# Three attention steps between the projection tiles of layer 0, and sums of squares that stay on TensorE

## The chip, the cores and the metric

One core of one Trainium2 chip runs the program. Its engines work from queues of their own: TensorE (PE, with its weight loads shown as PEld), VectorE (DVE), ScalarE (ACT), GpSimd (POOL) and the queue that issues transfers (SP). The metric is device microseconds of one execution, the median of three runs: 2119.75 (2119.36 to 2120.94).

## The reference, cut to what matters

Two layers (DEPTH 2) over 512 latent tokens with 256 context tokens ahead of them, 1024 wide. Each layer: adaLN modulation, RMSNorm, one input projection for three head groups, an output projection, then SwiGLU. The three groups are latent attention (mla, 4 heads), neighbourhood attention (na, 4 heads of 64) and a bidirectional gated DeltaNet (4 heads of 128). The parts that the change touches:

```
def l2_norm(x):
    return xf * lax.rsqrt(jnp.sum(xf * xf, axis=-1, keepdims=True) + EPS)

# gated_deltanet_mixer, for latents and for context:
qkv = silu(centred_depthwise_conv(t[..., :3 * DN_W], conv_w))
g = -exp(a_log) * softplus(a + dt_bias)
return l2_norm(q), l2_norm(k), v, g, sigmoid(b)

# chunk_gated_delta_rule, chunks of 64 tokens:
gc = cumsum(g)
decay = exp(gc_i - gc_j)                  # lower triangle
L = strict_lower(kb @ k.T) * decay        # kb = k * beta
tinv = inverse(L + I)
... a scan over the chunks with tinv, k_tail, q_dec and a_intra

# the gate projection z enters at the very end:
out = rms_norm(o, g_out) * silu(z)
```

## The kernel before, in words

A tile framework orders the instructions of each engine by simulating a timeline, within the order of the program text, data, and the buffers of its pools. Every large product is fp32 split in two parts: a weight tile is loaded (raw tile wr, two buffers, line 215), ACT casts its high part wh (line 216), POOL subtracts for the low part wl (line 217), and PE makes three products (hh with wh, hl with wh, hh with wl). Projections land in PSUM tiles acc_in (512 latent and 256 context columns of a head at a time).

The modulation columns (ada_cols, lines 222 to 242) load a tile wada, which has the same tag and the same two buffers as wr, multiply it (acc_ada), copy the row adarow and turn it by two small products (tr_ada). In layer 0, 24 of them run beside attention: two for each of the 12 steps (ADA).

A layer goes: the decay and gate inputs; then projections and convolutions of the DeltaNet's keys (conv, whose silu products dn_k are lines 504 and 506); norms("k"); the gates of six token chunks (each has k_tp, gram, dp on PE; gul, Ec on POOL; E on ACT); values, q and norms("q"); na's keys, queries and values; and the tail.

The order around the change:

- g (scal) comes off a DVE chain of softplus steps (lines 539 to 547). Five matmuls turn it into cumulative decays (tile gc, line 104 by the profile, since every mm has that line), then exps on ACT.
- norms (lines 568 to 591): ACT squares a head (sqd). PE multiplies it with a 32-column selector as the stationary operand, so that each head's sums land as rows of a PSUM tile (ssq). DVE copies the rows (line 581), PE transposes them by blocks of 128 (ss_tp, line 585), DVE copies each result into the statistics (stq or st4, line 586).
- After the gates, strips of the triangular matrices go through DRAM (d_inv); inverse(x) builds the block inverses from them: mix (transposes on DVE), pp and yq (products on PE), p, X and Y (copies).
- The tail of projections follows the string TAIL: z a gate projection tile (do_z, head by head), k the latent attention's key and value tile, q its query tile with ms_q (mean squares of sqs), n one step of neighbourhood attention (s_na scores, softmax, tp_na transposes copied to pt, o_na). Layer 0 has "zzzzkq", layer 1 "kznqznznz".
- A loop then runs the remaining attention steps, each with DNS[l] steps of the DeltaNet scan (yp, sp, oa) and, in layer 0, two modulation columns.

Of the kernel before, what the change touches and what calls it, by code (L numbers as in the profile page):

```python
# [9 lines left out]
F32 = mybir.dt.float32  # L10
F32R = mybir.dt.float32r
AF = mybir.ActivationFunctionType
ALU = mybir.AluOpType
# [4 lines left out]
P = 128  # L18
# [16 lines left out]
BN = dict(S=2, T=3)  # L35
BM = dict(S=3, T=3)
ADA = ([2] * 12, [])
DNS = ([1, 0, 0] + [1] * 4 + [0] + [1] * 12, [2, 2, 2, 1, 1, 2, 3] + [2] * 11)
ADA_T = "T"
EB = dict(e=5)  # L40
BO = {512: 3, 256: 2}
EB_TAG = {}
PRE0, LATE = True, ()
ROW = lambda S, V: S.copy
HLP = ([(k, 1) for k in range(8)], [], [(k, 1) for k in (0, 2, 4, 6, 7)], [])
TAIL = ["zzzzkq", "kznqznznz"]
INV = ((4, 3), (4, 3))
WV = ((6,), (23,))
MR = 2
# [51 lines left out]


def mm(nc, out, lhsT, rhs, start=True, stop=True):
    nc.tensor.matmul(out, lhsT, rhs, start=start, stop=stop)  # L104


def mm3(nc, out, l, r, start=True, stop=True):
# [255 lines left out]
def layer(tc, nc, a, l, es_x, xT, env, nx):  # L363
# [185 lines left out]
    S.activation(out=beta, in_=ab[:, :, 8:16], func=AF.Exp, scale=-1.0)  # L549
    V.tensor_scalar(out=beta, in0=beta, scalar1=1.0, scalar2=None, op0=ALU.add)  # L550
    V.reciprocal(out=beta, in_=beta)

    egc, etail, egl = sc6(), sc6(), sc6()
    tp = eb("gc")
    gf = g.rearrange("p c x -> p (c x)")
    for i, nm in enumerate(("u_f", "u_b", "v_f", "v_b", "ones")):
        mm(nc, tp[:, 48 * i:48 * i + 48], C(nm), gf)
    tpv = lambda i: tp[:, 48 * i:48 * i + 48].rearrange("p (c x) -> p c x", x=8)
    for d in range(2):
        ds_ = slice(4 * d, 4 * d + 4)  # L560
        S.activation(out=egc[:, :, ds_], in_=tpv(d)[:, :, ds_], func=AF.Exp)
        S.activation(out=etail[:, :, ds_], in_=tpv(2 + d)[:, :, ds_], func=AF.Exp)
    S.activation(out=egl, in_=tpv(4), func=AF.Exp)
    V.tensor_scalar(out=sml[:, 12:13], in0=sml2[:, 19:20], scalar1=0.5, scalar2=None, op0=ALU.mult)

    t2 = lambda nm: sb.tile([P, 512], F32, tag="t2", name=nm, bufs=5)

    def norms(nm, t_, stat, rk, w_ctx):

        cs = both if w_ctx else (LAT,)  # L570
        ps_ = [eb(f"ssq{ci}") for ci in range(len(cs))]
        for h in range(4):
            for ci, cols in enumerate(cs):
                w = cols.stop - cols.start
                sq = t_("sqd")
                S.activation(out=sq[:, :w], in_=hv[nm](h)[:, cols], func=AF.Square)
                mm(nc, ps_[ci][32 * h:32 * h + 32, 0:w], C("sel0"), sq[:, :w])
        rows = [t_(f"ssq_{ci}") for ci in range(len(cs))]
        for ci, cols in enumerate(cs):
            w = cols.stop - cols.start  # L580
            V.tensor_copy(out=rows[ci][:, 0:w], in_=ps_[ci][:, 0:w])
        n = 6 if w_ctx else 4
        for c in range(n):
            tp = eb("ss_tp")
            PE.transpose(tp[:, 0:P], rows[c // 4][:, (c % 4) * P:(c % 4 + 1) * P], ident)
            V.tensor_copy(out=stat[:, c], in_=tp[:, 0:P].rearrange("p (h x) -> p h x", h=4)[:, :, 0])
        V.tensor_scalar(out=stat[:, 0:n], in0=stat[:, 0:n], scalar1=EPS, scalar2=None, op0=ALU.add)
        S.activation(out=rk[:, 0:n], in_=stat[:, 0:n], func=AF.Ln)
        S.activation(out=rk[:, 0:n], in_=rk[:, 0:n], func=AF.Exp, scale=-0.5)

# [1 line left out]
        conv("k", h, kT[:, h])  # L592
    st4, rk = [sb.tile([P, 6, 4], F32, name=nm) for nm in ("st4", "rk")]
    norms("k", t2, st4, rk, True)
    irk = sc3()
    tt(out=irk, in0=st4, in1=rk, op=ALU.mult)
    rk2 = sc3()
# [249 lines left out]
    def attention():  # L847
        for pair in range(2):
            gm = gms[pair]
            o_na = sn.tile([P, T], F32, tag="o_na", name="o_na", bufs=1)  # L850
            grid = lambda t: t[:, LAT].rearrange("p (r c) -> p r c", c=GW)
            qh, ql, kh, kl = nqh[:, pair], nql[:, pair], nkh[:, pair], nkl[:, pair]
            for qt in range(nT // P):
                is_ctx = qt >= 4
                tok = slice(qt * P, (qt + 1) * P)
                c0 = (0, 8, 24, 32, 0, 0)[qt]
                var = (0, 1, 1, 2, 0, 0)[qt]
                vb = ((0, 1), (6, 7), (7, 8), (2, 3), (), ())[qt] + (4, 5)
                lo_ = 256 if is_ctx else 0
                pts = []  # L860
                for j in range(2):
                    hs = slice(64 * j, 64 * j + 64)
                    cutk = lambda t: grid(t)[hs, :, c0:c0 + 32].rearrange("p r (b c) -> p b r c", b=2)
                    s_ = att_bank("s_na")
                    if not is_ctx:
                        mm3(nc, s_[:, 0:256], (qh[hs, tok], ql[hs, tok]), (cutk(kh), cutk(kl)))
                    mm3(nc, s_[:, 256:512], (qh[hs, tok], ql[hs, tok]), (kh[hs, CTX], kl[hs, CTX]))
                    st_ = sn.tile([P, 8], F32, tag="st", name="st", bufs=4)
                    pr = sn.tile([P, 512], F32, tag="pr", name="pr", bufs=2)
                    V.reduce_max(out=st_[:, 0:1], in_=s_[:, 256:512], axis=AX.X)  # L870
                    if is_ctx:
                        V.tensor_scalar(out=st_[:, 2:3], in0=st_[:, 0:1], scalar1=-1.0, scalar2=None, op0=ALU.mult)
                    else:
                        V.tensor_tensor_reduce(out=pr[:, 0:256], in0=s_[:, 0:256], in1=gm[:, j, var].rearrange("p b r c -> p (b r c)"),
                                               scale=1.0, scalar=NEG, op0=ALU.add, op1=ALU.max, accum_out=st_[:, 1:2])
                        V.tensor_scalar(out=st_[:, 2:3], in0=st_[:, 0:1], scalar1=st_[:, 1:2], scalar2=-1.0, op0=ALU.max, op1=ALU.mult)
                        S.activation(out=pr[:, 0:256], in_=pr[:, 0:256], func=AF.Exp, bias=st_[:, 2:3], accum_out=st_[:, 3:4])
                    S.activation(out=pr[:, 256:512], in_=s_[:, 256:512], func=AF.Exp, bias=st_[:, 2:3], accum_out=st_[:, 4:5])
                    if is_ctx:
                        V.reciprocal(out=st_[:, 5:6], in_=st_[:, 4:5])  # L880
                    else:
                        tt(out=st_[:, 6:7], in0=st_[:, 3:4], in1=st_[:, 4:5], op=ALU.add)
                        V.reciprocal(out=st_[:, 5:6], in_=st_[:, 6:7])
                    V.tensor_scalar(out=pr[:, lo_:512], in0=pr[:, lo_:512], scalar1=st_[:, 5:6], scalar2=None, op0=ALU.mult)
                    tp = att_bank("tp_na")
                    nb = 2 if is_ctx else 4
                    for b in range(nb):
                        o2 = lo_ + b * P
                        PE.transpose(tp[:, b * P:(b + 1) * P], pr[:, o2:o2 + P], ident)  # L889
                    pt = sn.tile([P, 512], F32, tag="pt", name="pt", bufs=3)  # L890
                    (S.copy if j == 0 else V.tensor_copy)(out=pt[:, 0:nb * P], in_=tp[:, 0:nb * P])
                    pts.append(pt)
                o_ = att_bank("o_na")
                for b in range(len(vb)):
                    for j in range(2):
                        hd = 2 * pair + j
                        mm(nc, o_[j * 64:j * 64 + 64, 0:P], nav[:, vb[b], hd * 64:hd * 64 + 64], pts[j][:, b * P:(b + 1) * P],
                           b == 0, b == len(vb) - 1)
                if is_ctx:
                    S.copy(out=o_na[:, tok], in_=o_[:, 0:P])  # L900
                else:
                    S.copy(out=grid(o_na)[:, :, 16 * qt:16 * qt + 16], in_=o_[:, 0:P].rearrange("p (r c) -> p r c", c=16))
                if qt == nT // P - 1:
                    nc.sync.dma_start(out=d_o[2 + pair][:, 0:nT], in_=o_na[:, 0:nT])
                    if l == 0 and e.dbg is not None and "na" in e.dbg:
                        nc.sync.dma_start(out=e.dbg["na"][:, pair], in_=o_na)
                yield True
# [74 lines left out]
    if "n" in TAIL[l]:  # L982
        open_na()
    z = iter(range(4))
    tail = dict(k=do_kv, q=do_ql, z=lambda: do_z(next(z)), n=lambda: next(na))
    for i in TAIL[l]:
        tail[i]()
    es_i.close()
# [84 lines left out]
    def finish(c, tok, o):  # L1073
# [13 lines left out]
        for h in range(4):  # L1087
# [4 lines left out]
    I_, S_ = (lambda x: lambda: inverse(x, sb, eb)), (lambda d, x: lambda: scan(d, x))  # L1092
    dn = iter([S_(0, 0), S_(1, 1), S_(0, 1), S_(1, 0), I_(2), S_(0, 2), S_(1, 3), I_(4), es_v.close,
               S_(0, 4), S_(1, 5), S_(0, 5), S_(1, 4), S_(0, 3), S_(1, 2)])
    dn_n, ada_n = iter(DNS[l]), iter(range(3 * KD))

    ada_bank = lambda name: (psV if ADA_T == "i" else psD).tile([P, 512], F32, tag=ADA_T, name=name, bufs=1)

    def beside(ada, sb):

        for _ in range(next(dn_n, 16)):
            next(dn, lambda: 0)()
        for _ in range(next(ada, 0) if l == 0 else 0):
            i = next(ada_n)
            e.ada_cols(0, (2, 4, 3)[i // KD], i % KD, 1, att_bank if ADA_T == "T" else ada_bank, sb, e.wp)

# [358 lines left out]
```

## Time and profile before

| what | value |
|---|---|
| median of 3 runs | 2119.75 us |
| the profiled execution | 2125.45 us, span 2123.6 us |
| mean granted clock of TensorE | 0.968 of full speed |
| PE busy | 1990.2 us, 94% |
| DVE, ACT, POOL busy | 55%, 34%, 36% |
| layer 0: key norms and gates; tail; loop | about 76 to 167; 264 to 372; 372 to 485 us |
| layer 1: key norms and gates; query norm | about 1294 to 1388; 1420 to 1433 us |

The page has the busy shares, the waits name for each idle stretch of an engine what ended it, the windows give busy time and granted clock of a stretch, the timeline gives single instructions. Idle time counts where PE has it, because PE is busy nearly all the time. The granted clock is 1.00 at 2.4 GHz and 0.5 at 1.2 GHz; a window's mean lies between.

### The profile page before, as it was taken

Reading aid. Unit: us, or ns where it says so; the run is one execution under the profiler, and the core shown is the slowest. Engines: PE = TensorE matmul, PEld = TensorE weight load, DVE = VectorE, ACT = ScalarE, POOL = GpSimd, SP = SyncE. Lnnn points to the kernel's source line nnn. Section 1 sums busy time; section 2 is a strip of 40 time slices with the busy share of each in tenths; the row PEclk is TensorE's granted clock in tenths of the full one; section 3 lists DMA queues with packets and bytes.
Section 4 is the critical chain, followed back from the end, with each engine's and each line's share of the span. In section 5 each row is a group of like instructions: output and inputs, shape, how many; then the busy total and the mean of one; then the engine's idle time right before and its main releaser. Section 6 shows DMA issues by size and latency. Waiting matters only on the chain. (4 is left out here: it accounts for less than half of the span.)

```text
span 2123.6 us, 32023 instructions
## 1 busy us (share of the span) xinstructions
PE 1990.2 (94%) x12770; PEld 1684.4 (79%) x12770; DVE 1172.3 (55%) x2045; ACT 714.3 (34%) x1385; POOL 758.7 (36%) x540
## 2 busy tenths in 40 slices
PE   6999998998998999999999988888998889999998
PEld 4788787887787888888888876767787678888887
DVE  4888813667656457246443268894568753212123
ACT  5433322334544221122122244333434543222233
POOL 3466132104322222322222443823311353444444
PEclk9999998999999999999999999999999999999999
DMA  7324252543322345344442331334232231333332
GB/s 279 82 76 153 81 157 77 168 149 112 104 64 78 109 126 165 97 130 131 128 129 76 121 95 55 119 120 124 91 88 77 87 95 60 99 99 94 95 97 92
DMA packets 119309, 232.56 MB, mean 110 GB/s; under 512 B 30516, under 2 KB 55988, under 8 KB 119032
## 3 DMA queue, kind: packets, MB, share of 16 engines
q1 hardware_dynamic: 119160, 230.51, 34.9%
q8 instruction: 101, 1.65, 0.3%
q14 instruction: 48, 0.39, 0.1%
HBM read 199.46 MB, written 31.01 MB: 109 GB/s over the span
## 5 line engine op out<-in xcount | busy, mean ns | idle before, releaser
L217 POOL TENSOR_TENSOR wl<-wr,wh 128x1024 fp32r<-128x1024 f32 (+2 forms) x188 | 442.0, 2352 | 848.4 <-ACT wh L216 834.9
L216 ACT CAST wh<-wr 128x1024 fp32r<-128x1024 f32 (+2 forms) x190 | 193.5, 1019 | 713.0 <-PE acc_gu L104 287.6
L104 PE MATMUL acc_gu<-fh,wh 128*128 128x512 f32 (+1 forms) x1024 | 359.1, 353 | 9.5 <-ACT fh L304 8.7
L104 PE MATMUL acc_gu<-fl,wh 128*128 128x512 f32 (+1 forms) x1024 | 361.0, 353 | 4.1 <-DVE fl L305 4.1
L104 PE MATMUL acc_gu<-fh,wl 128*128 128x512 f32 (+1 forms) x1024 | 360.2, 352 | 0.0
L104 PE MATMUL acc_in<-hh,wh 128*128 128x512 f32 (+1 forms) x640 | 230.5, 364 | 18.6 <-ACT xp L491 6.9
L104 PE MATMUL acc_in<-hl,wh 128*128 128x512 f32 (+1 forms) x640 | 229.9, 360 | 3.2 <-DVE hl L305 2.0
L104 PE MATMUL acc_in<-hh,wl 128*128 128x512 f32 (+1 forms) x640 | 227.3, 359 | 3.4 <-POOL wl L217 3.4
L104 PEld LDWEIGHTS acc_gu<-fh,wh 128*128 128x128 f32 x1024 | 194.1, 190 | 37.5 <-ACT fh L304 10.9
L1348 DVE TENSOR_TENSOR av<-acc_gu,av 128x768 f32<-128x768 f32 (+1 forms) x44 | 36.3, 825 | 338.4 <-PE acc_gu L104 330.0
L104 PEld LDWEIGHTS acc_gu<-fl,wh 128*128 128x128 f32 x1024 | 195.0, 190 | 30.3 <-DVE fl L305 4.3
L104 PEld LDWEIGHTS acc_gu<-fh,wl 128*128 128x128 f32 x1024 | 194.9, 190 | 26.3
L104 PEld LDWEIGHTS acc_in<-hh,wh 128*128 128x128 f32 x640 | 126.1, 198 | 45.4 <-ACT xp L491 8.6
L104 PE MATMUL acc_d<-al,wh 128*128 128x512 f32 (+1 forms) x444 | 157.2, 354 | 0.0
L104 PE MATMUL acc_d<-ah,wh 128*128 128x512 f32 (+1 forms) x444 | 157.2, 354 | 0.0
L104 PE MATMUL acc_d<-ah,wl 128*128 128x512 f32 (+1 forms) x444 | 156.1, 354 | 0.0
L254 DVE CUSTOM_DVE_ANT_0 junk<-wada,scb 128x1024 f32<-128x1024 f32 x112 | 145.3, 1297 | 6.8 <-DMA wada<-w_adaT 4.0
L104 PEld LDWEIGHTS acc_in<-hl,wh 128*128 128x128 f32 x640 | 127.0, 198 | 25.2 <-DVE hl L305 4.6
L104 PEld LDWEIGHTS acc_in<-hh,wl 128*128 128x128 f32 x640 | 126.1, 198 | 22.8 <-POOL wl L217 4.7
L1366 DVE SCALAR_TENSOR_TENSOR xT<-acc_d,mod,xT 128x512 f32<-128x512 f32 (+1 forms) x76 | 46.5, 634 | 155.2 <-PE acc_d L104 155.2
L501 DVE SCALAR_TENSOR_TENSOR cy<-xp,cw,cy 128x770 f32<-128x770 f32 (+1 forms) x96 | 117.7, 1226 | 20.5 <-ACT cy L499 18.5
L1352 DVE TENSOR_TENSOR al<-av,ah 128x768 fp32r<-128x768 f32 (+1 forms) x44 | 100.4, 2282 | 35.1 <-ACT ah L1351 35.1
(391 smaller groups left out, 3857.0 us busy)
## 6 DMA issues: line engine op xcount, KB each, us to landing
wr<-w_gu SPq DMA_DIRECT2D x88, 512.0 KB, 3.5
wada<-w_adaT SPq DMA_DIRECT2D x56, 512.0 KB, 3.4
wr<-w_in SPq DMA_DIRECT2D x48, 512.0 KB, 3.6
wr<-w_dn SPq DMA_DIRECT2D x32, 448.0 KB, 3.3
wada<-w_ada SPq DMA_DIRECT2D x24, 512.0 KB, 3.4
wada<-w_ada SPq DMA_DIRECT2D x8, 1024.0 KB, 8.1
wr<-w_dn SPq DMA_DIRECT2D x16, 512.0 KB, 3.5
xT<-xT SPq DMA_DIRECT2D x16, 384.0 KB, 4.9
```

What stands on the lines that cost most here:

```text
L104: nc.tensor.matmul(out, lhsT, rhs, start=start, stop=stop)
L216: S.copy(out=hi[:, sl], in_=raw[:, sl])
L217: eng.tensor_tensor(out=lo[:, sl], in0=raw[:, sl], in1=hi[:, sl].bitcast(F32), op=ALU.subtract)
L254: V.tensor_tensor_reduce(out=junk, in0=w, in1=scb[:, s], scale=1.0, scalar=0.0, op0=ALU.mult, op1=ALU.add, accum_out=mod[l][:, part, j, s: ...
L501: stt(out=y[:, :wid], in0=xp[:, j:j + wid], scalar=w_(j), in1=y[:, :wid], op0=ALU.mult, op1=ALU.add)
L1348: tt(out=av[:, :nT], in0=accs[1][:, :nT], in1=av[:, :nT], op=ALU.mult)
L1352: after.append(tt(out=l_[:, :nT], in0=av[:, :nT], in1=h_[:, :nT].bitcast(F32), op=ALU.subtract))
L1366: stt(out=xT[:, m, st_], in0=acc, scalar=mod[l][:, 5, m, s:s + 1], in1=xT[:, m, st_], op0=ALU.mult, op1=ALU.add)
```

## The change

Four edits:

1. TAIL[0] becomes "zknzqnznz": three of the 12 attention steps of layer 0, each with its two modulation columns, stand between the tail's tiles. The loop keeps nine. DNS[0] has one DeltaNet step beside every step of it. The choice of another PSUM bank for the columns, which was not in use, goes.
2. norms: every 128-column block of the squares is itself the stationary operand, with two columns of ones as the moving one. The sums land as columns, tokens along partitions. The row copies, transposes and copies of statistics go; DVE adds EPS straight from PSUM.
3. The five gc matmuls and their exps stand behind norms("k"), with the last ssq matmul as the point after which they are issued.
4. pt has two buffers in layer 0 and three in layer 1, as against three in both.

```diff
-DNS = ([1, 0, 0] + [1] * 4 + [0] + [1] * 12, [2, 2, 2, 1, 1, 2, 3] + [2] * 11)
+DNS = ([1] * 20, [2, 2, 2, 1, 1, 2, 3] + [2] * 11)
-TAIL = ["zzzzkq", "kznqznznz"]
+TAIL = ["zknzqnznz", "kznqznznz"]
...
+    def norms(nm, t_, stat, rk, w_ctx):
+        ps_, n = eb("ssq"), 6 if w_ctx else 4
+        for h in range(4):
+            for cols in both if w_ctx else (LAT,):
+                w = cols.stop - cols.start
+                sq = t_("sqd")
+                S.activation(out=sq[:, :w], in_=hv[nm](h)[:, cols], func=AF.Square)
+                for i in range(w // P):
+                    o = 2 * (4 * (cols.start // P + i) + h)
+                    e.last["ssq"] = mm(nc, ps_[:, o:o + 2], sq[:, i * P:(i + 1) * P], C("ones")[:, 0:2])
+        sums = ps_[:, 0:8 * n].rearrange("p (c h s) -> p c h s", h=4, s=2)[:, :, :, 0]
+        V.tensor_scalar(out=stat[:, 0:n], in0=sums, scalar1=EPS, scalar2=None, op0=ALU.add)
...
+    norms("k", t2, st4, rk, True)
...
-    for i, nm in enumerate(("u_f", "u_b", "v_f", "v_b", "ones")):
-        mm(nc, tp[:, 48 * i:48 * i + 48], C(nm), gf)
+    with tc.issue_after(e.last["ssq"].ins):
+        for i, nm in enumerate(("u_f", "u_b", "v_f", "v_b", "ones")):
+            mm(nc, tp[:, 48 * i:48 * i + 48], C(nm), gf)
...
-        rows = [t_(f"ssq_{ci}") for ci in range(len(cs))]
-            V.tensor_copy(out=rows[ci][:, 0:w], in_=ps_[ci][:, 0:w])
-            PE.transpose(tp[:, 0:P], rows[c // 4][:, (c % 4) * P:(c % 4 + 1) * P], ident)
-            V.tensor_copy(out=stat[:, c], in_=tp[:, 0:P].rearrange("p (h x) -> p h x", h=4)[:, :, 0])
...
-                    pt = sn.tile([P, 512], F32, tag="pt", name="pt", bufs=3)
+                    pt = sn.tile([P, 512], F32, tag="pt", name="pt", bufs=2 + l)
...
+    def modulations(ada, sb, bank):
+        for _ in range(next(ada, 0) if l == 0 else 0):
+            i = next(ada_n)
+            e.ada_cols(0, (2, 4, 3)[i // KD], i % KD, 1, bank, sb, e.wp)
+    def step_na():
+        modulations(ada, sn, att_bank)
+        next(na)
-    tail = dict(k=do_kv, q=do_ql, z=lambda: do_z(next(z)), n=lambda: next(na))
+    tail = dict(k=do_kv, q=do_ql, z=lambda: do_z(next(z)), n=step_na)
```

On PE, in layer 1's key part (acc_in are projection products, gc the decays, ssq the sums of squares), this stands before:

```order
L104 MATMUL acc_in<-hh_10598,wl 128x512
L104 MATMUL gc<-scal,cst_61 128x48 x4
L104 MATMUL gc<-scal,cst 128x48
L104 MATMUL ssq_11662<-sqd,cst_61 32x512
L104 MATMUL ssq_11663<-sqd,cst_61 32x256
L104 MATMUL ssq_11662<-sqd,cst_61 32x512
L104 MATMUL ssq_11663<-sqd,cst_61 32x256
L104 MATMUL ssq_11662<-sqd,cst_61 32x512
```

And now:

```order
L103 MATMUL acc_in<-hl_10590,wh 128x512
L103 MATMUL ssq<-cst,sqd 128x2 x6
L103 MATMUL gc<-scal,cst_61 128x48 x4
L103 MATMUL gc<-scal,cst 128x48
L610 MATMUL k_tp<-cst_61,dn_k 128x128 x4
L103 MATMUL gram<-dn_k 128x128 x4
L103 MATMUL dp<-guh,cstR 128x512
L103 MATMUL dp<-gul,cstR 128x512
L103 MATMUL dp<-cstR 128x512
```

The decays stood ahead of the sums, behind 168 units of 512 projection columns since the layer's gate inputs; now they stand behind all 24 blocks of the sums and 185 units, and the first chunk's gate (k_tp, gram, dp) follows at once, which stood behind 232 units before.

On PE, at the end of layer 0's tail, this stood before (acc_in the last projection tile, ms_q the query's mean squares, yp the first product of the scan):

```order
L104 MATMUL acc_in<-hh_128,wl 128x256
L104 MATMUL ms_q<-cst,sqs 128x2 x6
L104 MATMUL tr_ada<-cst,adarow 128x2
L104 MATMUL acc_ada<-wada,sc 32x128 x8
L104 MATMUL yp<-vp,Y_2572 128x128 x4
L104 MATMUL pp<-mix,LP 32x32 x4
```

And in the middle of the tail there is now, behind z0, the key and value tile and a first set of scores, in one run:

```order
L103 MATMUL ms_kv<-sq,cst 128x256
L103 MATMUL pp<-mix,LP 32x32 x32
L103 MATMUL pp<-p_2562,strips 32x32 x16
L103 MATMUL pp_2582<-X,LP 64x64 x8
L103 MATMUL yq<-strips,p_2562 32x32 x11
L103 MATMUL pp_2582<-X,LP 64x64 x8
L103 MATMUL yq<-strips,p_2562 32x32 x21
L103 MATMUL yq_2639<-Y_2558,p_2599 64x64 x8
L103 MATMUL acc_ada<-wada,sc 32x128 x8
L103 MATMUL yq_2639<-Y_2560,p_2599 64x64 x8
L103 MATMUL tr_ada<-cst,adarow 128x2
L103 MATMUL acc_ada<-wada,sc 32x128 x8
```

The inverse's pp and yq stood spread among the z tiles; now they stand together ahead of z1, with the first two modulation columns in and behind them.

On SP, in the same tail, before (strips feed the inverse, wr are projection weights, d_z is the gate's store):

```order
L215 DMA wr<-w_in 128x1024
L798 DMA d_z_431<-z 768x1x128
L215 DMA wr<-w_in 128x1024
L686 DMA strips<-d_inv_436 128x48x32
L922 DMA LP<-d_LP_434 128x512 x2
L798 DMA d_z_431<-z 768x1x128
L215 DMA wr<-w_in 128x1024 x2
```

And now:

```order
L224 DMA wada<-w_ada 128x1024
L792 DMA d_z_431<-z 768x1x128
L224 DMA wada<-w_ada 128x1024
L680 DMA strips<-d_inv_436 128x48x32
L916 DMA LP<-d_LP_434 128x512 x2
L214 DMA wr<-w_in 128x1024 x3
L224 DMA wada<-w_ada 128x1024
```

Two loads of modulation columns have taken the place of the two weight loads ahead of the strips; z1's weights stand behind them, in the same two buffers.

## Rows read from the trace of the kernel before

**Rows 1.** Page, part 1: busy us, share of the span, instructions; all engines.

```profile
PE 1990.2 (94%) x12770; PEld 1684.4 (79%) x12770; DVE 1172.3 (55%) x2045; ACT 714.3 (34%) x1385; POOL 758.7 (36%) x540
```

**Rows 2.** Waits of PE, layer 1's convolution part, 1290 to 1430: us, times, longest.

```profile
PE gc L104 <- DVE scal L547: 6.7, 1, 6.7
PE acc_in L104 <- ACT xp L491: 5.0, 2, 4.2
PE ss_tp L585 <- DVE ssq L581: 3.0, 1, 3.0
...
PE s_na L104 <- DVE stq L586: 1.8, 1, 1.8
```

**Rows 3.** Windows, same part: length, busy of each engine, granted clock, DMA share, GB/s.

```profile
1294.10:1307.10 13.00, 6.39 (x24) 3.96 (x24) 12.65 (x21) 4.91 (x13) 5.35 (x5) 0.61 0.12 45
...
1343.00:1387.60 44.60, 39.17 (x234) 33.37 (x232) 35.40 (x34) 10.53 (x16) 36.94 (x30) 1.00 0.46 138
...
1420.00:1433.40 13.40, 8.04 (x44) 7.01 (x45) 13.16 (x28) 1.98 (x4) 2.37 (x1) 0.75 0.31 100
```

**Rows 4.** Timeline of DVE, layer 1: start, duration, engine, line, operation.

```profile
1300.45 0.21 DVE L547 TENSOR_TENSOR scal<-scr,ea 128x48 f32<-128x48 f32 x1
1300.57 0.68 DVE L504 SCALAR_TENSOR_TENSOR dn_k<-th,cy 128x512 f32<-128x512 f32 x1
```

**Rows 5.** Timeline of PE, layer 1's key norms, 1293 to 1325.

```profile
1312.06 1.48 PE L104 MATMUL ssq<-sqd,cst 128*32 128x512 f32 x4
1313.47 0.50 PE L104 MATMUL acc_in<-hh,wh 128*128 128x512 f32 x1
...
1314.73 0.39 PE L104 MATMUL acc_in<-hh,wl 128*128 128x512 f32 x1
1314.96 0.39 PE L104 MATMUL acc_in<-hh,wh 128*128 128x512 f32 x1
...
1319.27 0.71 PE L585 MATMUL ss_tp<-cst,ssq 128*128 128x128 f32 x5
```

**Rows 6.** Timeline of PE, layer 1's query squares of another head group.

```profile
1496.32 1.05 PE L104 MATMUL ms_q<-cst,sqs 128*128 128x2 f32 x8
1497.24 0.48 PE L104 MATMUL acc_in<-hh,wl 128*128 128x512 f32 x1
```

**Rows 7.** Tile ms_q, its weight loads: ns min/median/max, first to last start.

```profile
L104 PEld LDWEIGHTS ms_q<-cst,sqs x20: 186/333/338, 347.9 to 1497.1; 128*128 128x128 f32 x20
```

**Rows 8.** Waits of PE, layer 0's tail, 280 to 372.

```profile
PE tr_ada L104 <- DVE adarow L231: 4.3, 2, 3.8
PE ms_q L104 <- DVE sqs L775: 3.5, 1, 3.5
```

**Rows 9.** Windows, layer 0's tail and the attention loop behind it.

```profile
340.60:371.80 31.20, 22.66 (x135) 19.70 (x134) 17.55 (x46) 6.79 (x23) 11.14 (x8) 0.67 0.36 113
371.80:484.50 112.70, 112.66 (x1428) 94.81 (x1426) 75.15 (x244) 37.49 (x128) 15.72 (x22) 1.00 0.51 162
```

**Rows 10.** Waits of PE, layer 0's convolution part, 50 to 150.

```profile
PE acc_in L104 <- ACT xp L495: 1.3, 1, 1.3
```

**Rows 11.** Tile strips in layer 0, its load: issue, and us to landing.

```profile
L686 SPq DMA_DIRECT2D strips<-d_inv x1: 377/377/377, 281.0 to 281.0; - x1
...
DMA to landing us min/median/max: 7.8/7.8/7.8
```

**Rows 12.** Timeline of DVE, layer 0's tail: transposes of strips.

```profile
288.91 1.84 DVE L929 STREAM_TRANSPOSE mix<-strips 32x256 f32<-32x256 f32 x4 [4.24 <-DMA strips<-d_inv]
```

**Rows 13.** Timeline of PE, layer 0's tail: first products of the inverse.

```profile
295.09 1.91 PE L104 MATMUL pp<-mix,LP 32*32 32x32 f32 x64
```

**Rows 14.** Timeline of ACT, layer 1: a table load and what follows.

```profile
1327.55 1.28 ACT L588 ACT_TABLE_LOAD   x1
1328.85 0.22 ACT L588 ACTIVATE rk<-st 128x24 f32<-128x24 f32 x1
```

**Rows 15.** Page, part 6: loads of projection weights: count, KB each, us to landing.

```profile
wr<-w_in SPq DMA_DIRECT2D x48, 512.0 KB, 3.6
```

More of the change, by code (lines that the diff above doesn't have):

```diff
@@ L37 @@
 ADA = ([2] * 12, [])
-DNS = ([1, 0, 0] + [1] * 4 + [0] + [1] * 12, [2, 2, 2, 1, 1, 2, 3] + [2] * 11)
-ADA_T = "T"
+DNS = ([1] * 20, [2, 2, 2, 1, 1, 2, 3] + [2] * 11)
 EB = dict(e=5)
@@ L103, in mm @@
 def mm(nc, out, lhsT, rhs, start=True, stop=True):
-    nc.tensor.matmul(out, lhsT, rhs, start=start, stop=stop)
+    return nc.tensor.matmul(out, lhsT, rhs, start=start, stop=stop)
 def mm3(nc, out, l, r, start=True, stop=True):
@@ L551, in layer @@
     V.reciprocal(out=beta, in_=beta)
+    V.tensor_scalar(out=sml[:, 12:13], in0=sml2[:, 19:20], scalar1=0.5, scalar2=None, op0=ALU.mult)
+    t2 = lambda nm: sb.tile([P, 512], F32, tag="t2", name=nm, bufs=5)
+    def norms(nm, t_, stat, rk, w_ctx):
[10 more added lines that the diff above has]
+        V.tensor_scalar(out=stat[:, 0:n], in0=sums, scalar1=EPS, scalar2=None, op0=ALU.add)
+        S.activation(out=rk[:, 0:n], in_=stat[:, 0:n], func=AF.Ln)
+        S.activation(out=rk[:, 0:n], in_=rk[:, 0:n], func=AF.Exp, scale=-0.5)
+    for h in range(4):
+        conv("k", h, kT[:, h])
+    st4, rk = [sb.tile([P, 6, 4], F32, name=nm) for nm in ("st4", "rk")]
+    norms("k", t2, st4, rk, True)
     egc, etail, egl = sc6(), sc6(), sc6()
@@ L563, in layer @@
     S.activation(out=egl, in_=tpv(4), func=AF.Exp)
[L564 to L577, printed above, removed]
-        rows = [t_(f"ssq_{ci}") for ci in range(len(cs))]
-        for ci, cols in enumerate(cs):
-            w = cols.stop - cols.start
-            V.tensor_copy(out=rows[ci][:, 0:w], in_=ps_[ci][:, 0:w])
-        n = 6 if w_ctx else 4
-        for c in range(n):
-            tp = eb("ss_tp")
-            PE.transpose(tp[:, 0:P], rows[c // 4][:, (c % 4) * P:(c % 4 + 1) * P], ident)
-            V.tensor_copy(out=stat[:, c], in_=tp[:, 0:P].rearrange("p (h x) -> p h x", h=4)[:, :, 0])
-        V.tensor_scalar(out=stat[:, 0:n], in0=stat[:, 0:n], scalar1=EPS, scalar2=None, op0=ALU.add)
-        S.activation(out=rk[:, 0:n], in_=stat[:, 0:n], func=AF.Ln)
-        S.activation(out=rk[:, 0:n], in_=rk[:, 0:n], func=AF.Exp, scale=-0.5)
-    for h in range(4):
-        conv("k", h, kT[:, h])
-    st4, rk = [sb.tile([P, 6, 4], F32, name=nm) for nm in ("st4", "rk")]
-    norms("k", t2, st4, rk, True)
     irk = sc3()
@@ L984, in layer @@
     z = iter(range(4))
-    tail = dict(k=do_kv, q=do_ql, z=lambda: do_z(next(z)), n=lambda: next(na))
+    ada_n = iter(range(3 * KD))
+    def modulations(ada, sb, bank):
[6 more added lines that the diff above has]
+    tail = dict(k=do_kv, q=do_ql, z=lambda: do_z(next(z)), n=step_na)
     for i in TAIL[l]:
@@ L1094, in layer @@
                S_(0, 4), S_(1, 5), S_(0, 5), S_(1, 4), S_(0, 3), S_(1, 2)])
-    dn_n, ada_n = iter(DNS[l]), iter(range(3 * KD))
-    ada_bank = lambda name: (psV if ADA_T == "i" else psD).tile([P, 512], F32, tag=ADA_T, name=name, bufs=1)
+    dn_n = iter(DNS[l])
     def beside(ada, sb):
@@ L1102, in beside @@
             next(dn, lambda: 0)()
-        for _ in range(next(ada, 0) if l == 0 else 0):
-            i = next(ada_n)
-            e.ada_cols(0, (2, 4, 3)[i // KD], i % KD, 1, att_bank if ADA_T == "T" else ada_bank, sb, e.wp)
+        modulations(ada, sb, att_bank)
     while True:
```

## The prediction

> **What bounds the kernel now.** The page's table of busy times comes first: TensorE (PE) works for 94% of the span [rows 1], so every saving has to come out of the remaining 6%, out of PE work that goes, or out of PE work that ran at the lower clock. The change touches four places: key norms and query norms of both layers, and layer 0's tail (its last projection tiles). For each I read PE's waits, then the windows around them, then single instructions.
>
> Layer 1, key norms. PE waits 6.7 us for scal, the decay input g, written by line 547 on VectorE (DVE) [rows 2]. In the 13.0 us from 1294.1 PE is busy 6.39 us at a granted clock of 0.61 of 2.4 GHz [rows 3]. The reader is to see that DVE is full there (12.65 of 13.0) and that L547 ends only at 1300.66, just ahead of the last key head's product, L504 [rows 4]. PE sits at the decays' matmuls (gc), although the products and sums of squares behind them stand ready.
>
> Layer 1, later: the wait for xp (5.0 in two pieces), and around the query norm 3.0 us for the copied row of sums and 1.8 us for the statistics stq [rows 2]; 13.4 us there hold 8.04 us of PE work at clock 0.75 [rows 3].
>
> Layer 0, tail: PE waits 3.5 us for sqs (query squares) and 4.3 us for adarow (a modulation row) [rows 8]. The 31.2 us from 340.6 hold 22.66 us of PE work at clock 0.67; the attention loop behind, 112.66 of 112.70 us busy at full clock, has nothing to give [rows 9].
>
> **The change part by part.** Numbers are of the profiled execution (span 2123.6, time 2125.45), which is 5.7 us above the median of 2119.75; I subtract the gain from the median.
>
> 1. Sums of squares, PE work. Before, one head's 512 and 256 columns take 1.41 us (1312.06 to 1313.47), and five row transposes take 0.71 [rows 5]. Twelve heads at 1.41, and the four of layer 1's latent-only norm at two thirds of it, 0.94, are 16.9 + 3.8 = 20.7; 22 transposes at 0.14 are 3.1. Afterwards there are 88 blocks with a 128x128 stationary and 2 moving columns, each two instructions of the profile. The nearest row is ms_q, the same shape: eight instructions from 1496.32 to 1497.24, 0.115 each [rows 6]. 176 x 0.115 = 20.2. Saved: 3.6; I take 3.5. The other bound is that weight loads set the pace: 0.186 each at best [rows 7] makes 32.7, a cost of 8.9. The pitch of the same row, below its own loads' duration, puts me near the first.
>
> 2. Layer 1, key norms. gc moves behind the last sum of squares. Until there PE has 17 more units of 512 projection columns (185 against 168; 0.23 us each by the distance of two acc_in rows [rows 5], 3.9 us) and 18 blocks (4.1 us), so it arrives near 1302 instead of 1294. g, now behind the last head's DVE products, is late next: I leave 3 us of wait and of gul (POOL) behind gc, so 6.7 becomes about 3.7 gained. Clock: of 13.0 us at 0.61, 10.1 were at the half level; the idle time ends at 1300.7, so from 1297.0 some 3.7 of these were idle and 6.4 busy, 3.2 lost. 3.7 + 3.2 = 6.9. The chunks' gates now start 47 units earlier (185 against 232), which may bring the Bk chain forward, behind which ScalarE's (ACT) xp copies stand: 0 to 5.0 us. But gates load POOL, 36.94 of 44.6 us busy in their stretch [rows 3], and fewer projection columns lie beside them: I count 1.5.
>
> 3. Layer 1, query norm. Row copy, transposes and stq copies go, and the sums end before the v tiles. 3.0 + 1.8 idle [rows 2], and at 0.75 over 13.4 us half the time at the low level, 6.7 us, less those 1.8, is 4.9 of work, 2.4 lost: 7.2 in all. DVE stays nearly full (13.16 of 13.4), so something is late next: I leave 1.6 and take 5.6. Layer 1: 6.9 + 1.5 + 5.6 = 14, range 7 to 20.
>
> 4. Layer 0, key norms: the same move, where DVE is early. The xp wait behind gc is 1.3 [rows 10]. With what earlier statistics spare I take 2, bounds 0 to 4.
>
> 5. Layer 0, tail. Three attention steps, each with two modulation columns, now stand between z, k and q tiles. Going: 31.2 - 22.66 = 8.5 us of idle, and clock: at 0.67 some 20.6 us were at half; between 12.1 (all idle time inside) and 20.6 of it was work, so 6.1 to 10.3, I take 9. Together 17.5. Coming:
>  - inverse(0) (pp, yq) stood among z tiles; now it stands in one run behind z0, kv and a first set of scores, ahead of z1. Strips are issued at 281.01 and land 7.8 us later; their transposes mix end at 290.75 [rows 11, 12]. The old pp stood at 295.09 [rows 13] behind 32 more units, so PE now arrives about 287 to 290: up to 4 us of wait, 3 taken. Then its copies (ACT, DVE) lie uncovered, 3 us, and ACT has four table loads more, two of them ahead of the first copy p: 1.28 each [rows 14], 2.6, of which I count half.
>  - the first two weight loads of z1 share two buffers with the columns (tag wr) and on SP's queue wait for the first acc_ada, which stands behind inverse(0). A weight load lands in 3.6 us [rows 15] and is cast on ACT in about 1 us; PE has some 3 us of other work there. With restarts at half clock I take 5.5. Sum 3 + 3 + 1.3 + 5.5 = 12.8, bounds 6 (all but one load covered) and 46 (rival c).
>  - the new place of ms_q may still wait: 3 of the old 3.5. pt loses one of three buffers in layer 0 and the loop has fewer steps: 0 to 6, I take 2.
>  Tail: 17.5 - 12.8 - 3 - 2 = -0.3.
>
> Sum: 3.5 + 14 + 2 - 0.3 = 19.2. 2119.75 - 19.2 = 2100.6, forecast 2101.
>
> On the table loads: in the row, the operation behind a load of 1.28 us starts at once (1327.55 + 1.28 against 1328.85) [rows 14]. The Trainium skill, page "ScalarE: Activation LUTs", section "What ACT_TABLE_LOAD costs", gives about 1283 ns and a drain of 1380 ns, 2.66 us for a switch. The trace agrees with the first figure and shows no second. With the page's figure, the two ahead of p would cost 5.3 instead of 2.6, and the estimate would be some 1.4 us later at half counting.
>
> **Rivals.**
> (a) The waits change their names. In layer 1 gul and guh follow g immediately, and POOL, 83% busy in the gates' stretch, holds PE there; in the tail acc_ada's chain costs 5 more. Layer 1 gives 7, tail -5: 3.5 + 7 + 2 - 5 = 7.5, 2112. For it: POOL's share; against it: POOL was idle up to 1326 behind the first gul.
> (b) The tail's inverse lies hidden: PE arrives late enough and the queue is clear. Then most of the 12.8 is not paid: 2088. For it: eight units more and mix is there; against it: z1's weights can't be early.
> (c) Slower: the buffer ring in layer 0's tail. Weights and modulation columns take turns in two buffers; a column gives its buffer back only after its acc_ada, which needs a PSUM bank that inverse and attention share. At each of three steps a turn would cost a landing of 3.6, a cast of 1 and the subtraction on POOL, 2.4, twice less PE work beside it: about 12 each, 36, with half clock on 20 us of work behind them 46. 17.5 - 46 - 3 - 2 = -33.5; with 19.5 from the rest -14, so 2134. It makes the kernel slower when the tail's new waits pass 32 us (17.5 + 19.5 - 5). For it: SP's order itself; against it: such columns stood among the tail's tiles before, with 8.5 us of idle.
> (d) Loads set the pace of the sums of squares: 176 x 0.186 = 32.7 instead of 20.2, 12.5 more: 2113. Against it stands ms_q's pitch. The Trainium skill, page "Trainium Kernel Development and Optimization", section "Best Practices", says to judge TensorE by its weight loads' busy share and not by its matmuls'. By that rule this part of the change adds work, loads of 128 columns in place of 56 loads of 32.
> (e) The change leaves gc's wait as it is, since g is computed later: 6.9 and the gates' 1.5 fall away, and the tail loses 8: 2117.
>
> **How the numbers follow.** Forecast 0.50, (a) 0.20, (b) 0.14, (c) 0.07, (d) 0.04, (e) 0.05. The forecast's own range is 2094 to 2108. For eight in ten the range takes in (b) partly and (a): 2087 to 2114. A measurement of this kernel tells about 0.2% (4.2 us) from no change, so slower begins at 2124 and faster ends at 2115.5. Slower is (c), 0.07; the same are (e) and thirds of (a) and (d), rounded to 0.09; faster 0.84.
>
> **What would show it.** Right: gc's wait in layer 1 falls from 6.7 to 1 to 4 us; no wait for a copied row of sums; ssq's blocks with a pitch near 0.115; the stretch ahead of layer 0's attention loop at full clock without its 3.5 and 3.8; new waits of PE at pp for mix and at z1's acc_in for wh. Wrong: ssq's pitch near 0.19; dp waiting for gul by more than 6 us beyond before's; waits for wh or acc_ada of over 20 us in layer 0's tail; a loop in layer 0 with gaps before o_na.

## The result and the profile after

The change makes the kernel slower: 2148.26 us (median of 4 runs, 2133.66 to 2152.03) against 2120.35, a ratio of 1.0121 [1.0089, 1.0153]. The forecast was 2101. The profiled execution took 2149.12 us, span 2147.3, against a span of 2123.6 before.

PE's row of the page reads almost as before [rows 1]: still 94% of the span, but 24.4 us more in it, although the change takes work away.

```profile
PE 2014.6 (94%) x12868; PEld 1722.7 (80%) x12868; DVE 1172.9 (55%) x2016; ACT 719.2 (33%) x1389; POOL 760.1 (35%) x540
```

To see where it comes from, take the start of the same PE work in both traces (us from the start of the span):

| PE work | before | after | lead or lag |
|---|---|---|---|
| layer 0: first score s_na | 251.4 | 244.7 | -6.7 |
| layer 0: last o_na of the attention loop | 484.2 | 491.9 | +7.7 |
| layer 1: its first ab_tp (transposes of the gate inputs) | 1249.5 | 1254.9 | +5.4 |
| layer 1: first s_na | 1428.4 | 1432.0 | +3.6 |
| layer 1: last acc_in (end of the tail) | 1518.9 | 1525.3 | +6.4 |
| layer 1: last o_na of the loop | 1583.4 | 1606.5 | +23.1 |
| end | 2123.6 | 2147.3 | +23.7 |

Layer 0's convolutions gain 6.7, its tail and loop lose 14.4, layer 1's convolutions gain 1.8, and layer 1's attention loop loses 16.7. That last one is a stretch whose code the change does not touch. (The same program in another execution, e10_after_again, takes 243.2 us from the first score to the last o_na of layer 0, as against 247.2 here and 232.8 before: the tail and loop lose 10 to 14.)

The windows of PE in the two losing places, with the granted clock in the third number from the end: the inverse in layer 0's tail, the tiles behind it, layer 0's loop, layer 1's loop, and a part of that.

```profile
291.40:316.90 25.50, 23.03 (x288) 20.67 (x288) 7.13 (x22) 7.52 (x17) 6.86 (x4) 0.51 0.17 55
316.90:375.70 58.80, 57.24 (x382) 47.78 (x380) 15.14 (x43) 16.81 (x37) 8.93 (x6) 0.91 0.28 89
375.70:491.90 116.20, 111.31 (x1307) 94.18 (x1305) 75.08 (x224) 35.44 (x117) 25.54 (x28) 0.90 0.51 160
...
1525.30:1606.50 81.20, 79.50 (x764) 67.60 (x762) 42.58 (x116) 24.38 (x71) 17.73 (x15) 0.71 0.24 75
1535.00:1582.70 47.70, 47.66 (x353) 40.62 (x351) 20.52 (x59) 11.74 (x38) 6.42 (x6) 0.50 0.18 54
```

Read the last row first: 47.7 us with PE busy in 47.66 of them, and the clock at 0.50, the lower level, all the way. The stretch has no wait that a view of waits could name; its products take up to twice as long (eight instructions of sp 2.07 us, as against 1.16 before). Before, layer 1's loop took 64.5 us, with PE busy for 60.18 of them in 763 instructions at a mean clock of 0.95:

```profile
1518.90:1583.40 64.50, 60.18 (x763) 52.23 (x762) 43.18 (x116) 24.47 (x71) 17.77 (x15) 0.95 0.32 95
```

Now it is 764 instructions and 79.50 us of work. The inverse in layer 0 is the same picture, 25.5 us at 0.51.

How the first stretch begins, on PE's timeline of layer 0's tail:

```profile
286.00 0.70 PE L103 MATMUL ms_kv<-sq,cst 128*128 128x256 f32 x2 [1.45 <-ACT sq L748]
291.37 3.06 PE L103 MATMUL pp<-mix,LP 32*32 32x32 f32 x64 [4.67 <-DVE mix L923]
294.89 1.73 PE L103 MATMUL pp<-p,strips 32*32 32x32 f32 x32 [0.46 <-ACT p L942]
...
314.56 0.63 PE L103 MATMUL acc_in<-hl,wh 128*128 128x512 f32 x1
...
317.27 0.39 PE L103 MATMUL acc_in<-hh,wh 128*128 128x512 f32 x1
```

PE waits 4.67 us for mix, the strips' transposes. The strips themselves are there by 287.8, when POOL starts to read them; on DVE's queue kvn, the normed keys and values, stands ahead of mix and waits for ACT:

```profile
289.40 1.56 DVE L755 TENSOR_TENSOR kvn<-kvn,rs_kv 128x768 f32<-128x768 f32 x1 [4.39 <-ACT rs_kv L754]
290.89 1.83 DVE L923 STREAM_TRANSPOSE mix<-strips 32x256 f32<-32x256 f32 x4
```

Then 64 instructions (32 products of 32 by 32, two for each) take 3.06 us, as against 1.91 before [rows 13]. A projection product still takes 0.63 at 314.6, and 0.39 at 317.3, when the clock is back. In layer 1 it is a wait of 1.20 us for LP ahead of the same kind of products:

```profile
1534.76 2.52 PE L103 MATMUL pp<-mix,LP 32*32 32x32 f32 x48 [1.20 <-DMA LP<-d_LP]
```

A wait does not stand ahead of every fall. In layer 0's loop PE is busy throughout, at full clock up to 449.4, and at half from 449.5 to 459.6:

```profile
441.40:449.40 8.00, 8.00 (x114) 6.37 (x112) 5.76 (x18) 3.46 (x17) 1.63 (x4) 1.00 0.34 101
449.50:459.60 10.10, 10.10 (x69) 9.25 (x69) 5.26 (x14) 2.69 (x9) 1.04 (x1) 0.50 0.32 105
```

It has only small products there (s_na, pp, sp, ks, o_na, acc_ada). So the waits ahead of the two stretches are where the clock fell; that they are the reason isn't shown.

The convolution part of layer 1, PE's waits from 1250 to 1460, beside [rows 2]:

```profile
PE acc_in L103 <- ACT xp L490: 5.6, 3, 2.7
PE acc_in L103 <- DVE nkl L701: 3.4, 1, 3.4
PE acc_v L103 <- DVE nql L712: 3.3, 1, 3.3
PE dp L103 <- DVE LP L638: 3.2, 1, 3.2
PE dp L103 <- DVE st L568: 2.4, 1, 2.4
...
PE gc L103 <- DVE scal L546: 0.2, 1, 0.2
```

The waits that the prediction wanted gone are gone: gc's 6.7 is 0.2, and the transposes' 3.0 and 1.8 are no more. About as many have come: dp in the gates (8.3 us together, before 3.8), and 3.4 and 3.3 for nkl and nql (low parts of na's keys and queries), all behind DVE.

### The profile page after: what moved, and what is told of

Same layout as the page of the kernel before. It is cut to its first block, busy times and chain, and to the rows that moved or that the text cites. A ratio compares the mean times of both kernels' runs of the same rounds, so it can differ in the third digit from the quotient of the medians.

```text
span 2147.3 us, 32203 instructions
## 1 busy us (share of the span) xinstructions
PE 2014.6 (94%) x12868; PEld 1722.7 (80%) x12868; DVE 1172.9 (55%) x2016; ACT 719.2 (33%) x1389; POOL 760.1 (35%) x540
```

## The experiments

Three theories at first. C: the loss is work at half clock, which a short wait lets in and which lasts while PE has only small products. R: it is the tail's buffer ring (rival c). S, against C, says that the half clock comes from elsewhere and that dense work does not end it. Later two more on layer 1's loop: O, that its order decides, and L, that the stretch comes by chance in any order. Each kernel ran beside the kernel before on its chip: e1 to e4 on one, e5 to e8 on a second, e9 and e10 on a third.

| run | what it is | median us (runs) | ratio to before |
|---|---|---|---|
| e1_norms_gc | sums and decays, tail of before | 2128.46 (10) | 1.0049 [1.0020, 1.0077] |
| e2_tail | tail, DNS and pt alone | 2141.21 (4) | 1.0095 [1.0077, 1.0112] |
| e3_norms | sums alone | 2134.93 (6) | 1.0068 [1.0038, 1.0098] |
| e4_all_but_gc | the change, decays not moved | 2128.67 (5) | 1.0034 [1.0017, 1.0052] |
| e5_dense | the change and 32 dense products | 2156.24 (4) | 1.0163 [1.0134, 1.0193] |
| e6_no_cols_dense | e8_no_cols and 16 dense products | 2122.67 (10) | 1.0011 [0.9993, 1.0029] |
| e7_no_gul | the change without gul | 2125.76 (10) | 1.0018 [1.0001, 1.0035] |
| e8_no_cols | the change, no columns in the tail | 2129.34 (10) | 1.0031 [1.0004, 1.0057] |
| e9_order | e8_no_cols, layer 1's decays not moved | 2117.03 (12) | 0.9984 [0.9970, 0.9997] |
| e10_after_again | the change, unaltered | 2145.82 (9) | 1.0091 [1.0058, 1.0124] |

**The change in parts.** e1_norms_gc, with the tail of before:

```diff
-DNS = ([1] * 20, ...)
-TAIL = ["zknzqnznz", "kznqznznz"]
+DNS = ([1, 0, 0] + [1] * 4 + [0] + [1] * 12, ...)
+TAIL = ["zzzzkq", "kznqznznz"]
-pt = sn.tile(..., bufs=2 + l)
+pt = sn.tile(..., bufs=3)
```

> The sums of squares and the moved decays alone, layer 0's tail and attention loop as before. Theory C (the loss is PE work at the half clock, entered behind short gaps and kept while small products run): layer 0's convolution part keeps its gain of about 6.7 us, the 27 us at half clock behind the first pp are gone, and the layer 1 loop shows whether its 48 us at half clock belong to the norms' edit; time 2105 to 2115 without them, about 2130 with them. Theory R (the tail's buffer ring and waits carry the loss, rival c of the prediction): layer 1 is then not slower than before, time 2100 to 2110.

Layer 0 reaches its first score at 243.9, so the gain of its convolutions comes with the norms and decays, and not with the tail. The profiled run ends at 2120.0, but ten runs go from 2121.8 to 2148.1. In the profile layer 1's loop had little half clock (65.3 us), and even so 2121.8 is above the 2105 to 2115 that C allowed for. The stretch behind the first pp is gone, but one as long stands in layer 0 with the tail of before as well, behind the wait of 3.5 us for sqs ahead of the loop:

```profile
342.90:370.20 27.30, 22.24 (x126) 18.48 (x130) 14.36 (x44) 6.38 (x22) 8.58 (x5) 0.50 0.29 91
```

Before the change some 20.6 us there were at half [rows 9]. So half clock as such is not new in layer 0, but there is more of it: from the first score to the last o_na some 28 us before (232.8 us at a mean of 0.94), some 64 now (247.2 at 0.87). R's 2100 to 2110 is missed too.

e2_tail is the other half, the same lines the other way round, and the helpers, in the kernel before:

```diff
-TAIL = ["zzzzkq", "kznqznznz"]
+TAIL = ["zknzqnznz", "kznqznznz"]
...
-tail = dict(..., n=lambda: next(na))
+tail = dict(..., n=step_na)
```

> Layer 0's tail, DNS and pt alone; norms and decays as before, and with them PE's whole order in layer 1 behind the convolutions. Theory C: 14 us lost in layer 0 between the first pp and the last o_na, most of it as work at half clock (some 45 us of it there), and no long half-clock stretch in layer 1's loop, whose order is that of before: about 2130. Theory R: the loss is PE idle time in that tail, over 20 us, time 2140 or more, layer 1 unchanged.

From the first score to the last o_na it takes 241.0 us (254.2 to 495.2) against 232.8, with the inverse at 0.50:

```profile
297.10:322.80 25.70, 23.23 (x286) 21.01 (x288) 7.35 (x22) 7.74 (x18) 5.35 (x3) 0.50 0.18 54
1539.30:1603.30 64.00, 59.76 (x763) 51.92 (x762) 43.17 (x116) 24.47 (x71) 17.79 (x15) 0.95 0.32 95
```

Its second row is layer 1's loop, in PE's order of before: 64.0 us at 0.95. So the tail alone makes a loss, and it isn't the loss in layer 1. The median of 2141 is 11 above what C allowed for; in the profile the loss from first score to last o_na is 8.2, some 8 more arise between layer 0's loop and its SwiGLU (490 to 690), and their cause stays open.

e3_norms is e1_norms_gc with the decays' block back ahead of norms("k"):

```diff
+    for i, nm in enumerate(("u_f", "u_b", "v_f", "v_b", "ones")):
+        mm(nc, tp[:, 48 * i:48 * i + 48], C(nm), gf)
...
     norms("k", t2, st4, rk, True)
-    with tc.issue_after(e.last["ssq"].ins):
-        for i, nm in enumerate(("u_f", "u_b", "v_f", "v_b", "ones")):
-            mm(nc, tp[:, 48 * i:48 * i + 48], C(nm), gf)
```

> The sums of squares alone; decays where they stood, tail as before. Theory C: PE's work for the sums falls by about 3.5 us, the transposes' waits go (3.0 + 1.8 us in layer 1), gc's wait of 6.7 us stays: 2108 to 2116, unless a half-clock stretch of tens of us sits in layer 1's loop, then up to 2135. Theory R: 2108 to 2116 in any case.

Its profile has the stretch: 81.7 us for layer 1's loop at 0.71, in the order of the change although the decays have not moved. Six runs, 2128.8 to 2147.4.

e4_all_but_gc makes the same edit in the full change.

> The change without the decays' move: gc stands ahead of the sums again. If the move is worth what the prediction said (about 7 us in layer 1, 2 in layer 0), this is 2155 to 2160; Theory C: PE's order in layer 0 behind the convolutions is that of the change, so 50 us at half clock stay there; layer 1's loop has its own order and may or may not fall: 2130 to 2160.

It is faster than the change, 2126.2 to 2133.3, and not slower: its median of 2128.67 lies below both spans. The decays' move in layer 1 does remove gc's wait. But it changes more than that (next).

**Does dense work end a stretch?** e5_dense:

```diff
+        q64 = eb("pp64")
+        with tc.issue_after(first.ins):          # first: the last pp<-mix
+            for _ in range(16 if (l, x0) in ((0, 0), (1, 2)) else 0):
+                mm(nc, q64, e.R5["ident"], e.cstR[:, 0:512])
```

> The change, with 16 added dense products (128x128 stationary, 512 columns, results overwritten) right behind the first pp products, in layer 0's tail and in layer 1's loop: 3.6 us of PE work each at full clock, about 7 at half. Theory C (a fall of the clock behind a short wait lasts while PE has only small products, and dense ones end it): the 47.8 us at half clock of layer 1's loop and the 27.3 of layer 0's tail each shrink to about 7 to 14, and the time falls from 2148 to 2125 to 2138 although PE has 32 products more. Theory S (the half clock comes from load elsewhere or from chance, and dense work does not end it): the stretches stay, and the time rises to 2150 to 2162.

Its timeline in layer 0's tail, and the windows at the clock's changes, in layer 0 and in layer 1:

```profile
294.80 3.06 PE L103 MATMUL pp<-mix,LP 32*32 32x32 f32 x64 [6.11 <-DVE mix L923]
297.78 5.19 PE L103 MATMUL pp<-cstR 128*128 128x512 f32 x16
302.91 1.00 PE L103 MATMUL pp<-p,strips 32*32 32x32 f32 x29
```

```profile
294.80:300.60 5.80, 5.80 (x71) 5.16 (x72) 3.03 (x7) 0.83 (x2) 1.80 (x1) 0.50 0.01 3
300.60:307.40 6.80, 6.80 (x139) 6.00 (x137) 0.84 (x2) 1.45 (x4) 0.00 (x0) 1.00 0.01 2
1546.40:1566.90 20.50, 20.25 (x117) 17.00 (x118) 8.06 (x24) 4.40 (x13) 3.79 (x4) 0.50 0.17 52
1566.90:1602.30 35.40, 35.40 (x462) 30.91 (x461) 25.17 (x69) 12.54 (x40) 2.69 (x4) 1.00 0.18 56
```

In both places the clock rises while the dense products run, and PE was almost fully busy before and after. (In layer 1 they came only at 1563.1, ten us behind the last pp<-mix.) That much fits C. The rest does not. In layer 0 the small products of the inverse run at full clock for 6.8 us behind them; then it falls at 307.4, as a wait of 0.66 us for p begins and not behind it, and stays at half:

```profile
307.40:321.00 13.60, 12.77 (x97) 10.31 (x96) 5.09 (x15) 6.15 (x15) 3.21 (x2) 0.50 0.22 78
```

With 13.7 us at half before the rise (286.9 to 300.6) that makes 27.3, as much as without the dense products, and from the first score to the last o_na layer 0 takes 249.3 us instead of 247.2. The time is 2156 instead of C's 2125 to 2138, inside the 2150 to 2162 that S gave. Layer 1's loop fell from 81.2 to 67.2 us, but latent attention behind it (from its first score to its first output product), in an order that had changed, took 84.2 us instead of 75.6, and layer 0's 57.9 instead of 43.3. Why stays open; as a remedy the added products failed.

**What puts the inverse in one run?** e8_no_cols:

```diff
-ADA = ([2] * 12, [])
+ADA = ([0] * 3 + [3] * 6 + [2] * 3, [])
```

> The change without modulation columns in layer 0's tail: ADA is three zeros, then six times three and three times two, so that the three attention steps stay among the tiles and the loop has all 24 columns. The weights of z1 then no longer wait for a column's buffer. Rival c of the prediction and theory C agree on the tail: pp and yq stand among projection products again, no stretch of 27 us at half clock there, and from the first score to the last o_na of layer 0 it needs about 230 us instead of 247; layer 1 keeps its own chance of 48 us at half clock. Time 2105 to 2115 without it, 2125 to 2135 with it. If the columns are not what makes the inverse stand in one run, 27 us at half clock stay and the time is 2130 to 2150.

pp and yq stand among z1's products again, and the stretch from the first pp to ms_q is at full clock without a wait:

```profile
299.30:335.10 35.80, 35.80 (x395) 31.22 (x394) 11.26 (x25) 16.19 (x36) 9.02 (x4) 1.00 0.19 57
```

From the first score to the last o_na it is 231.1 us (245.2 to 476.3), 1.7 less than before the change and 16.1 less than with it (12.1 less than in e10_after_again). On SP two loads of z1's weights stand ahead of the strips again, as before the change. So the columns in the tail cost more than the three steps there bring; the loads' place in the queue is the likely way, and was not altered by itself. The profile ends at 2114.5; the ten runs go from 2112.4 to 2140.5.

e6_no_cols_dense adds the 16 products of layer 1 to that (the lines of e5_dense, with `range(16 if (l, x0) == (1, 2) else 0)`).

> The change without modulation columns in layer 0's tail (they run three or two beside the steps of the loop), and with the 16 dense products in layer 1's loop. Theory C: no long half-clock stretch in the inverse, since it stands among projection tiles again, and none in layer 1's loop: 2100 to 2118, faster than before. Theory S: as the version without the dense products, plus 4 us.

No gain in the median over before, C's 2100 to 2118 is missed, and so is S's 4 us more than e8_no_cols: in the profile the loop is still at half clock from 1509.6 to 1530.0, with PE busy throughout, and the clock rises as the dense products run. Yet the spread shrinks: 2117.4 to 2133.7, mean clock 0.962 to 0.967, where e8_no_cols has 0.953 to 0.969. The longest time is 7 us shorter than without the dense products, the shortest 5 us longer.

**Chance or order in layer 1's loop?** e10_after_again is the change itself.

> The change once more, unaltered, beside it on the same chip. If the stretch in layer 1's loop comes in some executions and not in others, its times spread over 20 us, as before (2134 to 2152), and its profile may or may not hold the 48 us; the 27 us at half clock in layer 0's inverse are there in any case.

Nine runs in two groups: four from 2123.9 to 2132.4 (clock 0.962 to 0.963) and five from 2145.8 to 2152.5 (0.951 to 0.956). This time the profile fell in the first; its inverse, and its layer 1 loop:

```profile
291.60:316.90 25.30, 22.79 (x286) 20.57 (x288) 7.11 (x21) 7.44 (x17) 6.79 (x4) 0.51 0.16 49
1524.00:1589.70 65.70, 63.38 (x763) 53.84 (x763) 42.68 (x116) 24.51 (x71) 17.77 (x15) 0.92 0.30 92
```

The same instructions, 65.7 us or 81.2. In both, the clock falls near 1535. Here it is back by the end of four yp at 1545.1, there the same yp run at half and it comes back only at 1582.7. So small products alone can also see the clock come back, which C as it was put leaves out. The inverse's 25 us are there both times.

e9_order keeps layer 0 of e8_no_cols and puts layer 1's decays ahead of the sums:

```diff
+    if l:
+        decays()             # the block with gc and its exps
...
     norms("k", t2, st4, rk, True)
+    if l == 0:
+        decays()
```

PE's loop there has the order of before: behind the wait come sp, ten pp, eight tp_na and four yp in a row; the change has six s_na behind sp, and pieces of pp between the tp_na.

> As the version without modulation columns in the tail, and in layer 1 the decays stand ahead of the sums again. That gives layer 1's loop the order that it has before the change (behind the first pp come sp, ten pp, eight tp_na and yp, and not six s_na and pieces of pp between); layer 0's order stays word for word. Theory O (the order behind the short wait decides whether the clock can stay at half for tens of us): no run has the 48 us at half clock, the runs lie within 10 us of each other, median 2112 to 2120, the fastest no faster than that version's 2112. Theory L (the stretch comes by chance in any order): runs spread over 20 us or more, median 2124 to 2132, as that version's 2112 to 2141.

Median 2117.03, faster than before by 0.16% [0.03%, 0.30%], which is less than the 0.2% that the prediction counts as no change, and 1.3% below the change beside it (2145.82): the best kernel here. Eleven of twelve runs lie in 2111.4 to 2120.5, one at 2126.4; the lowest mean clock is 0.961. The median is in O's span, but the spread of 15 us lies between O's 10 and L's 20. In its profile, layer 1's loop and the waits from 1250 to 1360:

```profile
1515.10:1579.10 64.00, 59.90 (x763) 51.90 (x762) 43.16 (x116) 24.50 (x71) 17.77 (x15) 0.95 0.32 95
```

```profile
PE gc L103 <- DVE scal L546: 6.7, 1, 6.7
```

The wait of 6.7 us for scal is back, and the kernel is faster with it. Profiles of this loop order (before, e2_tail, e4_all_but_gc, e9_order) have 64 to 65 us there, and their runs spread over 7 to 15 us; those of the other order (the change twice, e1_norms_gc, e3_norms, e8_no_cols) 65 or 81, over 18 to 29. That speaks for O, as far as such numbers go; e3_norms, with the decays not moved but in the other order, has the stretch, so the place of gc alone does not decide it. The order was not altered by itself, with all else equal.

**What sets the pace of layer 1's gates?** e7_no_gul leaves out the low parts of the decays:

```diff
-            for eng, g_, x_ in ((V, g_hl[0], "h"), (G, g_hl[1], "l")):
+            for eng, g_, x_ in ((V, g_hl[0], "h"),):
...
-            mm(nc, dp, e.R5["v_" + dn], gus[1], False, False)
```

> The change without gul: the low parts of the decays are left out (12 products on POOL of 1.4 us and 12 matmuls in each layer), so the output is less accurate. If POOL and DVE set the pace of layer 1's gates after the decays' move (POOL and DVE 24.3 and 24.4 us busy of 25), the waits for dp go, and from gc to the first value transpose layer 1 needs 48 to 53 us instead of 58.3. If they do not, it needs 56 to 58, 2 less for the matmuls left out.

From gc to the first value transpose 53.6 us (58.4 in the change, 59.5 in e8_no_cols), and the waits for dp end on DVE:

```profile
PE dp L103 <- DVE guh L625: 3.7, 2, 3.0
```

POOL fell from 49.3 to 34.1 us there, DVE from 52.5 to 45.6. It lands just outside the span expected for the first case and below the second. Of the 4.8 us less, 3.3 are PE's own work (49.59 to 46.25 us busy); its idle time fell only from 8.8 to 7.4, and no wait there ends on POOL in either. So DVE holds PE up in both; that POOL alone was a limit isn't shown. (Layer 1's loop had another order, without the stretch.)

## Why the prediction was wrong, point by point

1. Sums of squares on PE: right. The pitch was 0.105 (twelve from 1299.44 to 1300.70), not 0.19, so 176 take 18.5 us instead of the forecast 20.2, although each weight load lasts 192 ns. Rival (d), with its price of 0.186 each, falls. The twelve, and the product behind them:

```profile
1299.44 1.40 PE L103 MATMUL ssq<-cst,sqd 128*128 128x2 f32 x12
1300.70 0.48 PE L103 MATMUL acc_in<-hh,wl 128*128 128x512 f32 x1
```

The rule of the Trainium skill (page "Trainium Kernel Development and Optimization", section "Best Practices") judges TensorE by its weight loads' busy share, and that did rise, from 79% to 80% of the span. Whether loads that overlap set the pitch of 0.105, no run here separates.

2. Layer 1's key norms: the step "I count 1.5" for the earlier gates had the wrong sign, and the 3 us left for waits were too few. The waits for scal changed into waits for dp, as rival (a) has it, but they end on DVE, not on POOL's gul: PE reaches the gates before they are fed, with DVE 24.38 and POOL 24.32 of 25 us busy from 1320 to 1345. What the prediction held against (a), POOL idle up to 1326, was misread: two subtractions of 2.4 us stand on POOL there, at 1315 and 1321. Layer 1 gained 1.8 us up to its first score instead of 14.

3. Layer 1's query norm: the waits went, and 3.3 and 3.4 us for nql and nkl came, written by the same DVE queue. Between first score and end of the tail 2.8 us are given back.

4. Layer 0's key norms: 6.7 instead of 2 (with its share of the sums, some 4); e3_norms and e4_all_but_gc have it without the decays' move.

5. Layer 0's tail: the failed step is "Then its copies (ACT, DVE) lie uncovered, 3 us". The order of the inverse in one run had been read from the program, and the wait for mix was near in size (3 forecast, 4.67 measured), but by luck: the forecast had it from the landing of the strips, and it comes from kvn ahead of mix on DVE, behind rs_kv on ACT with two table loads of 1.28 us, at 283.7 and 287.2. The reload of z1's weights cost less than forecast, 0.7 for wh. What lies there is not a few copies but 25.5 us at half clock with 23.03 us of work, some 9 to 11 of them lost (an estimate, by 3.06 against 1.91 us for the same products and by half at most), and the 9 us that the prediction counted as won back from the clock ahead of the loop [rows 9] came again inside it, 116.2 us at 0.90, so some 23 of them at half. It priced the new run of small products at the full clock. Net -14.4 (-10.4 in e10_after_again) instead of -0.3. Rival (c) had the sign and the place, not the mechanism: the columns do hold z1's weights up, as order of the loads, while the wait for wh is 0.7 us.

6. Layer 1's loop was not in the sum at all: the prediction put it at nothing, without a reason. It takes 15.5 us more in one execution than in another of the same program (81.2 and 65.7), and the change turned its order into one in which that was seen. That makes most of the difference between 2130 and 2148. That the order is the cause is likely and not shown; why the clock stays low there stays open.

7. A slip that decided nothing: the chances for "the same", 0.05 and a third each of 0.20 and 0.04, come to 0.13, not 0.09.

## What to carry to other kernels

When a change puts small products in one run behind a wait, price them at the lower clock as well as at the full one: here such runs stood at half for 25 and for 48 us. PE's busy share doesn't show this, the granted clock does. A kernel whose order is set by a scheduler can change in places that the edit doesn't touch: compare the order there too, and time such a kernel several times before a profile is read as its typical run. In layer 1, where DVE and POOL were nearly full, the wait that was removed came back under another name.

## What was not expected of the hardware

A PE that was busy for 47.66 of 47.7 us stayed at 1.2 GHz throughout, and small products, 32 by 32 and 64 by 64, ran at full clock for 6.8 us behind 16 dense ones (e5_dense). The Trainium skill, page "TensorE: Matmul & The Clock Gate", section "HAM oscillation — how this bites in real kernels", explains the lower clock by waits for transfers between groups of matmuls. The fall in layer 1's loop stands behind such a wait, of 1.20 us for LP, but the wait of 4.67 us in layer 0 ends on DVE, and the fall at 449.5 stands behind none, with PE busy for all of the 8.00 us ahead of it. That the low clock then lasts for tens of us with no wait at all is not what the section describes either.
